# Keeping the transposed keys of a delta-rule layer for its recurrence, and giving one output half another tile's space

## The chip, the cores and the metric

The kernel runs on one core of one Trainium2 chip. The time is the device time of one execution in microseconds (us), the median of several runs. An engine is named as the profile names it: PE is the matrix engine, DVE the vector engine, ACT the scalar engine, POOL the general engine (GpSimd), SP the engine whose only work here is to issue transfers. A name with a q behind it (SPq, ACTq) is that engine's queue of transfers.

## The reference, cut to what matters

One decoder layer on 512 tokens of width 1024, all in float32. One input projection feeds two groups of heads, whose outputs go together through the output projection `w_out`; cross-attention, a SwiGLU block and a last norm follow.

```
u = rmsnorm(x) @ w_in
# group A, 4 heads of 128: q, k, v through a short convolution and silu; q, k normalised by head;
# decay g_cum and beta per token. In chunks of tokens:
a_mat = where(strict, beta * (k k^T) * decay, 0) + I          # lower triangular
u_c, w_c = solve(a_mat, [v * beta, k * beta * exp(g_cum)])
v_new = u_c - w_c state
o     = q_dec state + (q k^T * decay) v_new
state = state * last + k_dec^T v_new                          # k_dec = k * exp(g_last - g_cum)
# then a gated RMSNorm of o
# group B, 8 heads of 64: a score per (query, key), the best 128 keys of each query,
# softmax attention over those with a relative-position bias
h = x + concat(A, B) @ w_out
h = h + cross_attention(rmsnorm(h), mem);  h = h + swiglu(rmsnorm(h));  out = rmsnorm(h)
```

## The kernel before, in words

Four chunks of 128 tokens take the place of the reference's chunks of 64. Matmuls of full precision are made of three passes over pairs of a rounded tile and its rest (`wh`, `wl`, `XH`, `XL`, lines 149 to 151); most of PE's time goes to such passes.

Nobody writes an order of instructions by hand. The body is written as helpers in program order, and the tile framework runs a model of the engines over it and lays out each engine's list. So what stands next to what is decided by that planner, from the tiles that instructions read and write, and an edit of a few lines can change the lists far from where it stands. On the chip every engine takes its own list strictly in order.

PSUM, the matrix engine's output memory, has eight banks; in the first third they are divided into `g` (3 buffers), `lg` (2), `tp` (2) and `o` (1). A tile that names a `tag` shares its space with the other tiles of that tag and has to wait until they are no longer read.

The part that the change touches, group A, goes through these steps:

- `project` makes q, k and v of a head, by dense passes on PE and a convolution on DVE, ACT and POOL (lines 360 to 383). Beside it DVE runs `topk`, group B's selection: 16 rounds of a MAX8 and a MATCH_REPLACE for each of three score blocks (lines 486 and 487), then three fills (line 490).
- `prepare(h)` transposes the keys of head h on PE (`tokens`, line 634), squares them for the norm (`squares`, ACT), turns the norm into factors on POOL (`rsqrt`, whose power stands in line 234, and `kdc` in line 651), makes k k^T and q k^T on PE, and writes `NTt` and `A` on DVE (line 662). `NTt` goes to memory (line 665, `n_d`) by SP's queue.
- `diagonal_blocks` reads all 16x16 diagonal blocks back (line 678), inverts them on DVE by a chain of small operations (lines 688 to 707), writes them to `x_d` and `y_d` (line 709) and spreads them by eight transfers each into `X` and `Y` (line 714), which POOL has set to zero (lines 847 and 848).
- `level(0)`, `level(1)` and `last_level` build the full inverse from the blocks on PE and DVE (lines 723 to 755).
- `values_of` transposes the values (line 634 again) and `gates` makes the gate `zg` from the last four pairs of weights, split on POOL (line 142).
- `recurrence` goes over the chunks. Before the first it makes `ktok`, the keys with tokens in the partitions, times `kdc`: per head four transposes into the single buffer of bank `o` and one multiply on DVE (lines 765 to 769). A chunk uses `ktok` in line 778 for the state; its output is squared (line 811), scaled by POOL's power (line 234) and DVE (lines 813 to 818), transposed (line 822) and split into `OGh` and `OGl`.
- `attention` of group B runs in pairs of heads: copies `nath`, `natl` and transfers into `ks`, `kl`, `qs` (lines 562 to 572), logits (579, 580), a bias add and max (589), exp (591), transposes (595), their copy (597), then values (604) and row sums (613).

`ktok` has the tag `X`: it lies where `X` lay. `OGl` has the tag `OGl`, where `wu`, an early weight, lay. `Dm`, the decay factors that `prepare` reads, has the tag `X` too.

Of the kernel before, what the change touches and what calls it, by code (L numbers as in the profile page):

```python
# [10 lines left out]
FT = mybir.dt.float32  # L11
FR = mybir.dt.float32r
AF = mybir.ActivationFunctionType
OP = mybir.AluOpType
AX = mybir.AxisListType

T = 512
D = 1024
MEM = 256
NT = T // 128  # L20
# [61 lines left out]
def hybrid_block(ctx, tc, I, out):  # L82
    nc = tc.nc
    pe, act, dve, pool, sp = nc.tensor, nc.scalar, nc.vector, nc.gpsimd, nc.sync
# [19 lines left out]
    def pool_of(name, side=None):  # L104
        return tc.alloc_tile_pool(name=name, bufs=1, reuse_waits="tile", side=side) if side else \
            tc.alloc_tile_pool(name=name, bufs=1, reuse_waits="tile")
# [15 lines left out]
    def ps(tag="at"):  # L122
        n_ps[0] += 1
        if tag not in banks:
            turn[tag] = turn.get(tag, -1) + 1
            tag = alias[tag][turn[tag] % len(alias[tag])]
        return banks["pool"].tile([128, 512], FT, name=f"ps{n_ps[0]}", tag=tag, bufs=banks[tag])
# [5 lines left out]
    def t2k(shape=(128, 512), dt=FT):  # L133
        n_t[0] += 1
        return tmp.tile(list(shape), dt, name=f"t2k{n_t[0]}", tag="t2k", bufs=4)
# [45 lines left out]
    QK = [gdn.tile([128, 2, T], FT, name=f"QK{h}", tag=f"QK{h}") if h < 3 else None for h in range(4)]  # L181
# [45 lines left out]
    def small(n, dt=FT):  # L227
        n_small[0] += 1
        return held((128, n), f"sm{n_small[0]}", dt)
# [55 lines left out]
    for j in range(4):  # L285
        for t in range(NT):
            tt = slice(t * 128, (t + 1) * 128)
            for k in range(2):
                kk = 2 * j + k
                o = pu[t][:, :N_DSA]  # L290
# [5 lines left out]
    gp = pool_of("gp", "right")  # L296
# [12 lines left out]
    for t in range(NT):  # L309
# [17 lines left out]
        for d in range(2):  # L327
# [4 lines left out]
                          None, op0=OP.mult)  # L332
# [55 lines left out]
    for pr_ in range(4):  # L388
        q = ps()
# [48 lines left out]
    q = ps()  # L438
# [13 lines left out]
    for h in range(4):  # L452
        q = ps()
# [15 lines left out]
    q = ps()  # L469
# [151 lines left out]
        att.release()  # L621


    NTt = A = X = Y = None
    n_d = dram.tile([16 * 129, 128], FT, name="n_d")
    x_d = dram.tile([128, 256], FT, name="x_d")
    y_d = dram.tile([128, 256], FT, name="y_d")
    kdc, ssq_ = small(16), small(16)
    irk = {}

    def tokens(src, bank="g"):
        q = ps(bank)
        for c in range(NT):
            pe.transpose(q[:, c * 128:(c + 1) * 128], src[:, c * 128:(c + 1) * 128], ident)  # L634
        return q

    def squares(q, dst):
        j = t2k()
        for c in range(NT):
            act.activation(j[:, c * 128:(c + 1) * 128], q[:, c * 128:(c + 1) * 128], AF.Square,  # L640
                           accum_out=dst[:, c:c + 1])

    def prepare(h):
        hc = slice(4 * h, 4 * h + 4)
        rk, cc = small(4), small(4)
        irk[h] = small(4)
        squares(tokens(QK[h][:, 0, :]), rk)
        rsqrt(rk, rk, 1.0)
        pool.tensor_tensor(cc, rk, rk, op=OP.mult)
        pool.tensor_tensor(cc, cc, beta[:, hc], op=OP.mult)  # L650
        pool.tensor_tensor(kdc[:, hc], cc, kd[:, hc], op=OP.mult)
        dve.reciprocal(irk[h], rk)
        for c in range(NT):
            act.activation(Dm[:, h, c, :], Dm[:, h, c, :], AF.Identity, scale=cc[:, c:c + 1])
        for c2 in range(2):
            q = ps("g")
            for e in range(2):
                c = 2 * c2 + e
                pe.matmul(q[:, 256 * e:256 * e + 256], QK[h][:, 0, c * 128:(c + 1) * 128],
                          QK[h][:, :, c * 128:(c + 1) * 128], start=True, stop=True)  # L660
            for k, dst in enumerate((NTt, A)):
                dve.tensor_tensor(dst[:, h, 2 * c2:2 * c2 + 2, :],
                                  q.rearrange("p (e k i) -> p e k i", e=2, k=2)[:, :, k, :],
                                  Dm[:, h, 2 * c2:2 * c2 + 2, :], op=OP.mult)
        sp.dma_start(bass.AP(tensor=n_d.tensor, offset=n_d.offset + h * 66048,
                             ap=[[128, 128], [16512, 4], [1, 128]]), NTt[:, h])
        squares(tokens(QK[h][:, 1, :]), ssq_[:, hc])
        pool.tensor_tensor(QK[h][:, 1, :], QK[h][:, 1, :], row[:, h, :], op=OP.mult)
# [89 lines left out]
    def recurrence():  # L758

        sg, sg2 = small(16), small(16)  # L760
        rsqrt(sg, ssq_, 1.0)
        dve.tensor_scalar(sg, sg, float(np.float32(128 ** -0.5)), None, op0=OP.mult)
        dve.tensor_tensor(sg2, sg, sg, op=OP.mult)
        dve.tensor_scalar(sg2, sg2, 1.0 / 128, None, op0=OP.mult)
        ktok = gp.tile([128, 4, NT, 128], FT, name="ktok", tag="X")
        for h in range(4):
            q = tokens(QK[h][:, 0, :], "o")
            dve.tensor_tensor(ktok[:, h], q.rearrange("p (c d) -> p c d", c=NT),
                              kdc[:, 4 * h:4 * h + 4].unsqueeze(2).to_broadcast([128, NT, 128]), op=OP.mult)
        S = gp.tile([128, 4, 128], FT, name="S")  # L770
        yield
        for c in range(NT):
            cs = slice(c * 128, (c + 1) * 128)

            def heads(o, f):
                for h in range(4):
                    a_, b_ = f(h)
                    pe.matmul(o[:, h * 128:(h + 1) * 128], a_, b_, start=True, stop=True)  # L778

            Z = cv((128, 4, 128))  # L780
            O = ps("g")
            if c:
                q = ps("g")
                heads(q, lambda h: (QK[h][:, 0, cs], S[:, h, :]))

                for h in range(4):
                    pe.matmul(O[:, h * 128:(h + 1) * 128], QK[h][:, 1, cs], S[:, h, :], start=h == 0, stop=False)
                for h in range(4):
                    dve.scalar_tensor_tensor(Z[:, h, :], q[:, h * 128:(h + 1) * 128],
                                             negc[:, 4 * h + c:4 * h + c + 1], vtok[h][:, c, :], op0=OP.mult,  # L790
                                             op1=OP.add)
            q = ps("g")
            heads(q, lambda h: (Y[:, h, c, :], Z[:, h, :] if c else vtok[h][:, c, :]))
            V = cv((128, 4, 128))
            for h in range(4):
                act.activation(V[:, h], q[:, h * 128:(h + 1) * 128], AF.Copy)
            if c < NT - 1:
                q = ps("g")
                heads(q, lambda h: (ktok[:, h, c, :], V[:, h, :]))
                if c:  # L800
                    for h in range(4):
                        dve.scalar_tensor_tensor(S[:, h, :], S[:, h, :], last[:, 4 * h + c:4 * h + c + 1],
                                                 q[:, h * 128:(h + 1) * 128], op0=OP.mult, op1=OP.add)
                else:
                    dve.tensor_copy(S.rearrange("p h d -> p (h d)"), q)
            for h in range(4):
                pe.matmul(O[:, h * 128:(h + 1) * 128], A[:, h, c, :], V[:, h, :], start=not c and h == 0, stop=h == 3)
            so, fo = small(4), small(4)
            j = t2k()
            for h in range(4):  # L810
                act.activation(j[:, h * 128:(h + 1) * 128], O[:, h * 128:(h + 1) * 128], AF.Square,
                               accum_out=so[:, h:h + 1])
            dve.tensor_tensor(so, so, sg2[:, c::4], op=OP.mult)
            rsqrt(fo, so, 1.0)
            dve.tensor_tensor(fo, fo, sg[:, c::4], op=OP.mult)
            on = cv((128, 4, 128))
            for h in range(4):
                dve.scalar_tensor_tensor(on[:, h, :], O[:, h * 128:(h + 1) * 128], fo[:, h:h + 1],
                                         zg[c][:, h * 128:(h + 1) * 128], op0=OP.mult, op1=OP.mult)
            q = ps("g")  # L820
            for h in range(4):
                pe.transpose(q[:, h * 128:(h + 1) * 128], on[:, h, :], ident)
            split(OGh[:, :, cs], OGl[:, :, cs], q.rearrange("p (h i) -> p h i", h=4))
            yield
# [15 lines left out]
    xn.release()  # L840
    NTt = gp.tile([128, 4, NT, 128], FT, name="NTt", tag="NT")
    A = gp.tile([128, 4, NT, 128], FT, name="A", tag="A")
    for h in range(4):
        prepare(h)
    X = gp.tile([128, 4, NT, 128], FT, name="X", tag="X")
    Y = gp.tile([128, 4, NT, 128], FT, name="Y", tag="Y")
# [6 lines left out]
    for h in range(4):  # L853
        values_of(h)
    OGh = gp.tile([128, 4, T], FR, name="OGh", tag="NT")
    OGl = gp.tile([128, 4, T], FR, name="OGl", tag="OGl")
    core = recurrence()
    steps(core, 2)
    for i, _ in enumerate(attention()):
# [50 lines left out]
    for k in range(KD):  # L910
        q = ps()
# [138 lines left out]
    for f0, nf in ((0, 8), (8, 8)):  # L1050
        HT = [gated(f) for f in range(f0, f0 + nf)]
        for m in range(KD):
            wh, wl = weights(I["w_down"][0], f0, nf, m * 128, 128)
            o = dense(wh, wl, [a for a, _ in HT], [b for _, b in HT])
# [5 lines left out]
    for hf in range(2):  # L1060
        for t in range(NT):
            q = ps()
# [67 lines left out]
```

## Time and profile before

| | us |
|---|---|
| median of 3 runs | 844.17 (843.04 to 844.74) |
| the profiled execution | 844.85 |
| its span, first to last instruction | 843.1 |
| PE busy | 817.6 (97%) |
| DVE busy | 477.3 (57%) |
| ACT busy | 371.6 (44%) |
| POOL busy | 191.3 (23%) |

The times of the trace count from the span's start; 1.75 us of the profiled execution lie outside the span. An instruction's duration on PE includes a modelled end, so that back-to-back matmuls overlap in the list: their cost is read from one start to the next. A bracket behind a row gives how long the engine sat idle ahead of it and what ended that.

### The profile page before, as it was taken

What the parts mean: (1) busy time and instruction counts of PE and PEld (TensorE: products, weight loads), DVE (VectorE), ACT (ScalarE), POOL (GpSimd) and SP (SyncE); (2) the same over time, 40 slices, a digit from 0 to 9 for tenths busy, and PEclk for the clock granted to TensorE, in tenths of its full rate; (3) what the DMA queues carried; (4) which work ended last, traced back from release to release, by engine and by line L of the source; (5) the groups of instructions that cost most, each with busy time, mean ns of one, the idle gap of its engine ahead of it and who ended that gap; (6) DMA issues with size and microseconds to landing.
All of it is one profiled execution on the core that took longest, in us unless ns stands there. A gap on an engine that the chain in (4) does not pass through costs nothing.

```text
span 843.1 us, 11038 instructions
## 1 busy us (share of the span) xinstructions
PE 817.6 (97%) x4122; PEld 680.3 (81%) x4122; DVE 477.3 (57%) x817; ACT 371.6 (44%) x736; POOL 191.3 (23%) x202
## 2 busy tenths in 40 slices
PE   8999999879998999999999999999999999999996
PEld 7787788768886888888878888888888888888885
DVE  7779999936673654564644444544354553335542
ACT  6679767227675543453544342322233222223332
POOL 5432578662310231000003211110011110001122
PEclk9999999989999999999999999999999999999998
DMA  8541333057415334343323533323333333332202
GB/s 292 144 110 30 111 100 89 7 112 169 121 51 204 96 101 128 111 137 100 101 59 94 172 100 101 92 83 101 100 100 101 93 89 100 94 100 87 88 25 100
DMA packets 134941, 88.31 MB, mean 105 GB/s; under 512 B 10304, under 2 KB 122344, under 8 KB 134888
## 3 DMA queue, kind: packets, MB, share of 16 engines
q1 hardware_dynamic: 131848, 85.87, 35.0%
q10 hardware_dynamic: 3040, 1.75, 0.7%
q8 instruction: 32, 0.52, 0.3%
q14 instruction: 21, 0.17, 0.1%
HBM read 76.84 MB, written 4.99 MB: 97 GB/s over the span
## 4 chain that ended last, share of the span: by engine, by line
PE 87%; DVE 4%; ACT 4%; DMA 2%; issue 1%; POOL 0%; SPq 0%; POOLq 0%; DVEq 0%; ACTq 0%
PE ps L149 23%; PE ps L151 23%; PE ps L150 23%; PE ps L604 1%; PE ps L723 1%; PE ps L778 1%; PE ps L1075 1%; PE ps L1074 1%; PE ps L1073 1%; PE ps L595 1%; PE ps L951 1%; PE ps L949 1%; PE ps L950 1%; PE ps L731 1%; PE ps L634 1%
## 5 line engine op out<-in xcount | busy, mean ns | idle before, releaser
L141 ACT ACTIVATE wh<-wraw 128x1024 fp32r<-128x1024 f32 x120 | 127.2, 1061 | 322.3 <-PE ps L150 169.2
L151 PE MATMUL ps<-XH,wl 128*128 128x512 f32 x512 | 201.1, 393 | 0.0
L149 PE MATMUL ps<-XH,wh 128*128 128x512 f32 x512 | 200.4, 391 | 0.4 <-DVE cp L366 0.3
L150 PE MATMUL ps<-XL,wh 128*128 128x512 f32 x512 | 199.5, 390 | 0.0
L142 DVE TENSOR_TENSOR wl<-wraw,wh 128x1024 fp32r<-128x1024 f32 x108 | 153.7, 1424 | 68.2 <-ACT wh L141 67.9
L149 PEld LDWEIGHTS ps<-XH,wh 128*128 128x128 f32 x512 | 96.2, 188 | 20.3 <-DVE cp L366 0.8
L150 PEld LDWEIGHTS ps<-XL,wh 128*128 128x128 f32 x512 | 96.2, 188 | 20.1 <-issue 0.2
L151 PEld LDWEIGHTS ps<-XH,wl 128*128 128x128 f32 x512 | 96.1, 188 | 19.6
L1044 POOL TENSOR_TENSOR t2k<-t2k,t2k 128x512 f32<-128x512 f32 x22 | 29.4, 1335 | 291.0 <-DVE t2k L1043 281.8
L258 POOL TENSOR_TENSOR acc<-acc,t2k 128x512 f32<-128x512 f32 x21 | 36.6, 1741 | 172.5 <-ACT t2k L257 172.0
L1043 DVE TENSOR_TENSOR t2k<-ps,row 128x512 f32<-128x512 f32 x22 | 15.2, 691 | 67.9 <-PE ps L151 67.9
L151 PE MATMUL ps<-HH,wl 128*128 128x512 f32 x128 | 50.0, 393 | 0.0
L149 PE MATMUL ps<-HH,wh 128*128 128x512 f32 x128 | 49.9, 390 | 0.0
L150 PE MATMUL ps<-HL,wh 128*128 128x512 f32 x128 | 49.6, 390 | 0.0
L1055 DVE TENSOR_TENSOR XR<-ps,XR 128x512 f32<-128x512 f32 x16 | 11.1, 692 | 51.9 <-PE ps L151 51.9
L1041 DVE TENSOR_TENSOR t2k<-ps,row 128x512 f32<-128x512 f32 x22 | 15.2, 691 | 36.0 <-PE ps L151 36.0
L142 POOL TENSOR_TENSOR wl<-wraw,wh 128x1024 fp32r<-128x1024 f32 x12 | 29.0, 2420 | 15.3 <-ACT wh L141 15.3
L885 DVE TENSOR_TENSOR XR<-ps,XR 128x512 f32<-128x512 f32 x16 | 11.0, 690 | 32.1 <-PE ps L151 32.1
L150 PEld LDWEIGHTS ps<-HL,wh 128*128 128x128 f32 x128 | 24.0, 188 | 5.1
L151 PEld LDWEIGHTS ps<-HH,wl 128*128 128x128 f32 x128 | 24.0, 188 | 4.9
L149 PEld LDWEIGHTS ps<-HH,wh 128*128 128x128 f32 x128 | 24.1, 188 | 4.9
L486 DVE MAX8 m<-masks 128x8 f32<-128x512 f32 (+2 forms) x48 | 26.8, 558 | 0.9
(395 smaller groups left out, 1628.9 us busy)
## 6 DMA issues: line engine op xcount, KB each, us to landing
wraw<-in_w_gate SPq DMA_DIRECT2D x22, 512.0 KB, 3.6
wraw<-in_w_up SPq DMA_DIRECT2D x22, 512.0 KB, 3.7
wraw<-in_w_down SPq DMA_DIRECT2D x20, 512.0 KB, 3.8
wraw<-in_w_in SPq DMA_DIRECT2D x16, 512.0 KB, 3.6
wraw<-in_w_xkv SPq DMA_DIRECT2D x16, 512.0 KB, 3.8
wraw<-in_w_out SPq DMA_DIRECT2D x8, 512.0 KB, 3.9
wraw<-in_w_xq SPq DMA_DIRECT2D x8, 512.0 KB, 3.8
wraw<-in_w_xo SPq DMA_DIRECT2D x8, 512.0 KB, 3.7
```

Of the source, the lines that this page charges most:

```text
L141: act.activation(h, src, AF.Copy)
L142: (sub or dve).tensor_tensor(l, src, f32(h), op=OP.subtract)
L149: pe.matmul(o, lh, rh, start=start, stop=False)
L150: pe.matmul(o, lh, rl, start=False, stop=False)
L151: pe.matmul(o, ll, rh, start=False, stop=stop)
L258: pool.tensor_tensor(self.acc, self.acc, s_, op=OP.add)
L486: dve.max(m8, score[t])
L885: dve.tensor_tensor(XR[m], o, XR[m], op=OP.add)
L1041: dve.tensor_tensor(s1, og_, Rrow2, op=OP.mult)
L1043: dve.tensor_tensor(s2, ou_, Rrow2, op=OP.mult)
L1044: pool.tensor_tensor(s1, s1, s2, op=OP.mult)
L1055: dve.tensor_tensor(XR[m], o, XR[m], op=OP.add)
```

## The change

`prepare` keeps the transposed keys (`kt`, in bank `g`) until `kdc` is there, and multiplies them into `ktok` at once. `recurrence` no longer transposes the keys again. For that `ktok` has to be there earlier, and takes the tag `OGl`; `OGl` takes the tag `X`. Behind line 654 the changed kernel's line numbers are 3 higher than before, and behind the block that is taken out of `recurrence` 2 lower.

```diff
-    NTt = A = X = Y = None
+    NTt = A = X = Y = ktok = None
...
-        squares(tokens(QK[h][:, 0, :]), rk)
+        kt = tokens(QK[h][:, 0, :])
+        squares(kt, rk)
         rsqrt(rk, rk, 1.0)
...
         dve.reciprocal(irk[h], rk)
+        dve.tensor_tensor(ktok[:, h], kt.rearrange("p (c d) -> p c d", c=NT),
+                          kdc[:, hc].unsqueeze(2).to_broadcast([128, NT, 128]), op=OP.mult)
...
-        ktok = gp.tile([128, 4, NT, 128], FT, name="ktok", tag="X")
-        for h in range(4):
-            q = tokens(QK[h][:, 0, :], "o")
-            dve.tensor_tensor(ktok[:, h], q.rearrange("p (c d) -> p c d", c=NT),
-                              kdc[:, 4 * h:4 * h + 4].unsqueeze(2).to_broadcast([128, NT, 128]), op=OP.mult)
...
     A = gp.tile([128, 4, NT, 128], FT, name="A", tag="A")
+    ktok = gp.tile([128, 4, NT, 128], FT, name="ktok", tag="OGl")
...
-    OGl = gp.tile([128, 4, T], FR, name="OGl", tag="OGl")
+    OGl = gp.tile([128, 4, T], FR, name="OGl", tag="X")
```

The instruction counts of ACT, POOL, SP and DVE stay; PE has 16 transposes fewer. The lists are laid out anew from the first heads' `prepare` on, up to the start of `w_out`; from there PE's list is as before but for some transposes of the memory tokens, which stand earlier.

DVE around the last head's `NTt` and `A`. Before (`cv_1771` holds the diagonal blocks that have come back, `m_994` and `masks` are the selection's):

```order
L662 TENSOR_TENSOR NTt<-ps_1750,Dm 128x256
L662 TENSOR_TENSOR A<-ps_1750,Dm 128x256
L486 MAX m_994<-masks 128x8
L379 SCALAR_TENSOR_TENSOR cp_1416<-cp_1406,prT,ps_1409 128x512
L487 MATCH_REPLACE masks<-m_994,masks 128x512
L486 MAX m_994<-masks 128x8
L487 MATCH_REPLACE masks<-m_994,masks 128x384
L486 MAX m_994<-masks 128x8
L688 TENSOR_SCALAR cv_1771<-cv_1771 128x256
L487 MATCH_REPLACE masks<-m_994,masks 128x256
L486 MAX m_994<-masks 128x8
L487 MATCH_REPLACE masks<-m_994,masks 128x512
```

After, the same place (`ps_1729` holds the kept keys of head 3, `sm_920` is `kdc`, `cv_1776` holds the diagonal blocks):

```order
L654 TENSOR_TENSOR ktok<-ps_1729,sm_920 128x512
L486 MAX m_994<-masks 128x8
L665 TENSOR_TENSOR NTt<-ps_1750,Dm 128x256
L665 TENSOR_TENSOR A<-ps_1750,Dm 128x256
L665 TENSOR_TENSOR NTt<-ps_1755,Dm 128x256
L665 TENSOR_TENSOR A<-ps_1755,Dm 128x256
L487 MATCH_REPLACE masks<-m_994,masks 128x512
L486 MAX m_994<-masks 128x8
L487 MATCH_REPLACE masks<-m_994,masks 128x384
L486 MAX m_994<-masks 128x8
L487 MATCH_REPLACE masks<-m_994,masks 128x256
L486 MAX m_994<-masks 128x8
```

The last pair of `NTt` and `A` now stands behind four `ktok` multiplies, the convolution's line 379 and one round more of the selection (four MAX, three MATCH_REPLACE); behind line 691, the old 688, one round is left where there were two.

PE at the end of `level(0)`'s products. Before (`cv_1822` to `cv_1843` are the masked products of line 725, `qs_2163` and its like the queries of the first pair of attention heads):

```order
L723 MATMUL ps_1838<-X,NTt 128x128 x4
L731 MATMUL ps_1845<-Y,cv_1822 128x128 x4
L731 MATMUL ps_1851<-Y,cv_1829 128x128 x4
L731 MATMUL ps_1857<-Y,cv_1836 128x128 x4
L731 MATMUL ps_1863<-Y,cv_1843 128x128 x4
L634 MATMUL ps_1869<-cst,Y 128x128 x4
L634 MATMUL ps_1875<-cst,Y 128x128 x4
L634 MATMUL ps_1881<-cst,Y 128x128 x4
L634 MATMUL ps_1887<-cst,Y 128x128 x4
L723 MATMUL ps_1893<-X,NTt 128x128 x4
L579 MATMUL ps_2185<-kl_2163,qs_2161 128x128
L580 MATMUL ps_2185<-ks_2162,qs_2161 128x128
```

After:

```order
L734 MATMUL ps_1850<-Y,cv_1827 128x128 x4
L734 MATMUL ps_1856<-Y,cv_1834 128x128 x4
L579 MATMUL ps_2165<-kl_2143,qs_2141 128x128
L580 MATMUL ps_2165<-ks_2142,qs_2141 128x128
L734 MATMUL ps_1862<-Y,cv_1841 128x128 x4
L734 MATMUL ps_1868<-Y,cv_1848 128x128 x4
L579 MATMUL ps_2166<-kl_2143,qs_2141 128x128
L580 MATMUL ps_2166<-ks_2142,qs_2141 128x128
L634 MATMUL ps_1874<-cst,Y 128x128 x4
```

The first logits of attention have moved ahead of two products of `level(0)`, of its four groups of transposes and of the first product of `level(1)`, and with them all of attention against the inverse and the recurrence.

PE ahead of `w_out`. Before (`ps_2664` is the last chunk's output, `ps_2708` its transpose):

```order
L807 MATMUL ps_2664<-cv_2683,A 128x128 x4
L595 MATMUL ps_2856<-cst,sm_2_2852 128x128 x3
L595 MATMUL ps_2871<-cst,sm_3_2867 128x128 x4
L595 MATMUL ps_2881<-cst,sm_3_2877 128x128 x4
L604 MATMUL ps_2887<-PT_2769,vt_980 64x512
L613 MATMUL ps_2899<-cst,c_3_2796 64x128 x8
L604 MATMUL ps_2887<-PT_2772,vt_980 64x512
L604 MATMUL ps_2887<-PT_2769,vt_984 64x384
L604 MATMUL ps_2887<-PT_2772,vt_984 64x384
L604 MATMUL ps_2887<-PT_2769,vt_988 64x256
L822 MATMUL ps_2708<-cst,cv_2703 128x128 x3
L604 MATMUL ps_2887<-PT_2772,vt_988 64x256
```

After (`ps_2644` is the last chunk's output, `ps_2688` its transpose):

```order
L776 MATMUL ps_2658<-cv_2643,Y 128x128 x4
L604 MATMUL ps_2867<-PT_2749,vt_980 64x512
L613 MATMUL ps_2879<-cst,c_3_2776 64x128 x8
L604 MATMUL ps_2867<-PT_2752,vt_980 64x512
L604 MATMUL ps_2867<-PT_2749,vt_984 64x384
L604 MATMUL ps_2867<-PT_2752,vt_984 64x384
L604 MATMUL ps_2867<-PT_2749,vt_988 64x256
L805 MATMUL ps_2644<-cv_2663,A 128x128 x4
L604 MATMUL ps_2867<-PT_2752,vt_988 64x256
L604 MATMUL ps_2867<-PT_2749,vt_992 64x128
L604 MATMUL ps_2867<-PT_2752,vt_992 64x128
L820 MATMUL ps_2688<-cst,cv_2683 128x128 x4
```

In both lists `w_out`'s line 149 follows within five rows. The last chunk's output product (line 807, now 805) has moved behind five of the last pair's eight value products.

## Rows read from the trace of the kernel before

**Rows 1.** The page's busy times: engine, busy us, share of the span, instructions.
```profile
PE 817.6 (97%) x4122; PEld 680.3 (81%) x4122; DVE 477.3 (57%) x817; ACT 371.6 (44%) x736; POOL 191.3 (23%) x202
```

**Rows 2.** Windows: us of each engine (instructions), granted clock, share of DMA engines, GB/s.
```profile
120.00:140.00 20.00, 20.00 (x96) 16.62 (x95) 18.93 (x48) 13.60 (x37) 15.26 (x17) 1.00 0.33 93
```

**Rows 3.** Waits from 155 to 266 us: who waited for what, us, times, longest.
```profile
PE ps L723 <- DMA B<-tb_d: 5.6, 1, 5.6
PE ps L595 <- ACT PT L597: 1.5, 1, 1.5
PE ps L595 <- ACT sm L591: 1.4, 2, 1.0
```

**Rows 4.** Timeline of PE, level 0: start, us, line, tiles, count, [idle before].
```profile
177.44 6.51 PE L723 MATMUL ps<-X,NTt 128*128 128x128 f32 x32 [5.62 <-DMA B<-tb_d]
183.79 3.74 PE L731 MATMUL ps<-Y,cv 128*128 128x128 f32 x32
```

**Rows 5.** Timeline of DVE from the last `A` to the end of the blocks' inverse.
```profile
144.44 0.41 DVE L662 TENSOR_TENSOR A<-ps,Dm 128x256 f32<-128x256 f32 x1
...
149.93 1.24 DVE L688 TENSOR_SCALAR cv<-cv 128x256 f32<-128x256 f32 x1 [1.46 <-DMA cv<-n_d]
...
151.59 0.70 DVE L486 MAX8 m<-masks 128x8 f32<-128x512 f32 x1
...
155.35 0.69 DVE L486 MAX8 m<-masks 128x8 f32<-128x512 f32 x1
...
157.67 2.33 DVE L695 TENSOR_TENSOR cv<-cv,cv 128x12 f32<-128x12 f32 x1
...
160.44 1.88 DVE L692 TENSOR_TENSOR cv<-cv,cv 128x16 f32<-128x16 f32 x1
...
163.32 0.15 DVE L692 TENSOR_TENSOR cv<-cv,cv 128x12 f32<-128x12 f32 x1
...
168.99 0.39 DVE L707 COPY cv<-cv 128x256 f32<-128x256 f32 x1
```

**Rows 6.** Timeline of POOL in the same stretch.
```profile
144.11 2.42 POOL L142 TENSOR_TENSOR wl<-wraw,wh 128x1024 fp32r<-128x1024 f32 x1 [1.69 <-ACT wh L141]
...
154.45 2.92 POOL L234 TENSOR_TENSOR sm<-sm,mhalf 128x16 f32<-128x16 f32 x1
157.33 4.95 POOL L142 TENSOR_TENSOR wl<-wraw,wh 128x1024 fp32r<-128x1024 f32 x2
```

**Rows 7.** Timeline of SP's queue: time spent issuing.
```profile
169.03 0.34 SPq L709 DMA_DIRECT2D x_d<-cv  x1
...
170.77 4.29 SPq L714 DMA_DIRECT2D X<-x_d  x8
```

**Rows 8.** The same queue later: the first pair's queries.
```profile
185.07 1.18 SPq L571 DMA_DIRECT2D qs<-nath  x2
187.98 1.10 SPq L572 DMA_DIRECT2D qs<-natl  x2
```

**Rows 9.** Timeline of PE: the transposes for `ktok` and what follows them.
```profile
207.35 0.66 PE L634 MATMUL ps<-cst,QK 128*128 128x128 f32 x4 [0.27 <-DVE ktok L768]
...
211.10 0.66 PE L634 MATMUL ps<-cst,QK 128*128 128x128 f32 x4
211.51 0.36 PE L579 MATMUL ps<-kl,qs 128*128 128x256 f32 x1
```

**Rows 10.** Instructions on the tile `ktok`: durations min/median/max in ns, starts.
```profile
L768 DVE TENSOR_TENSOR ktok<-ps,sm x4: 676/692/692, 206.6 to 213.8; 128x512 f32<-128x512 f32 x4
```

**Rows 11.** Timeline of ACT, third chunk's end: squares of its output.
```profile
242.30 0.28 ACT L811 ACTIVATE t2k<-ps 128x128 f32<-128x128 f32 x1 [0.30 <-PE ps L807]
```

**Rows 12.** Timeline of DVE, third chunk's end: its output is scaled.
```profile
245.26 1.12 DVE L818 SCALAR_TENSOR_TENSOR cv<-ps,sm,zg 128x128 f32<-128x128 f32 x4
```

**Rows 13.** Windows behind PE's waits for the last pair.
```profile
258.00:260.00 2.00, 2.00 (x10) 0.90 (x12) 1.29 (x5) 0.60 (x1) 0.47 (x1) 0.55 1.07 363
260.00:262.00 2.00, 2.00 (x16) 1.59 (x15) 0.00 (x0) 0.53 (x1) 0.00 (x0) 0.60 0.97 355
```

**Rows 14.** Timeline of PE ahead of `w_out`.
```profile
252.80 1.05 PE L807 MATMUL ps<-cv,A 128*128 128x128 f32 x8
...
264.49 0.50 PE L149 MATMUL ps<-odh,wh 128*128 128x512 f32 x1
```

## The prediction

> **What bounds the kernel now.** I read the page's busy times first: PE works for 97% of the span and no other engine for more than 57% [rows 1]. So the time is PE's work plus the few places where PE waits or runs at the low clock, and an edit is worth what it does to those. The list of PE's waits comes next. In the stretch that the change lays out anew it has one large entry, 5.6 us at the first product of `level(0)`, and two of 1.5 and 1.4 us in the last pair of attention heads [rows 3]. The third view is the timeline around the large one: PE sits for 5.62 us and starts at 177.44 [rows 4]. Its releaser is given as a transfer of `B`, but eight transfers into `X` were issued just ahead of it on the same queue [rows 7]; what PE needs is `X`, and `X` is the end of a chain on DVE. So up to 177.44 us DVE sets the time and not PE. DVE is full there: 18.93 of 20 us between 120 and 140 us [rows 2]. From 177.44 us to the start of `w_out` at 264.49 us [rows 4, 14] PE sets the time again, with few gaps. Behind 264.49 PE's list is dense and stays.
>
> The sum thus has two parts: when `level(0)` starts, and how much PE work, waiting and low clock lies between that and `w_out`. I work it against the profiled execution, 844.85 us, which is 0.68 above the median of 844.17; a difference of a sum is carried over to the median as it is.
>
> **The transposes that go.** There are 16, in four groups of four. The first group ran before the wait at 177.44, where PE has time to spare: nothing gained. Three groups ran behind it. From the start of one to the next instruction is 0.41 us [rows 9], so 3 x 0.41 = 1.23 us, all on PE's path. One of the three waited 0.27 us for the multiply ahead of it, since bank `o` has one buffer [rows 9]; that goes too. Together -1.5 us.
>
> **The multiplies that move.** Four of about 0.69 us each [rows 10] leave the stretch from 206 to 214 us, where DVE has time, and go into the selection's, where it has none. The order has them all ahead of the last head's `NTt` and `A`, and with them one convolution step of about the same size and one more round of the selection. A round takes 155.35 - 151.59 = 3.76 us [rows 5]; a fourth MAX of 0.7 us comes with it. Together 4 x 0.65 (their spacing when queued, an estimate just under their duration) + 0.7 + 3.76 + 0.7 = 7.8 us, so the last `A` would end at 144.85 + 7.8 = 152.6 us. The low bound takes off what DVE idled, about 1 us in each 20 [rows 2] and some 3 us in all: 149.6. The high bound counts two rounds, the multiply and the four last products behind the last projection's eviction: about 155.
>
> Behind the last `A` the chain is shorter than before. Then: 144.85 to 168.99 + 0.39 = 169.38, or 24.5 us [rows 5]. Now: 5.1 us until the blocks are back (149.93 - 144.85), 1.24 for line 688, one round and three fills for some 3.9 us, since the other round is already done, and then the inversion without a round between its steps. From 163.32 to 169.38 it took 6.1 us, and the four small steps ahead of that need 0.1 each, 6.4 together. Sum 16.6 us. So the chain ends at 152.6 + 16.6 = 169.2 instead of 169.38: -0.2 us, with bounds of -3.2 and +2.6. The transfers behind it are the same, and two of `B` that now stand ahead of those into `X` on SP's queue fit into the 1.4 us in which that queue waits for `x_d` to land (169.37 to 170.77 [rows 7]). That these two shifts nearly cancel is the main point of the sum, and luck.
>
> Two of the chain's steps on a dozen numbers took 2.33 and 1.88 us, while the same step later took 0.15 [rows 5]. Both end when POOL's two weight splits end, 157.33 + 4.95 = 162.28 [rows 6]. My 6.4 us leaves such blocking out. In the new order one weight split follows `X`'s zeroing and the power of 2.92 us [rows 6] is last; counted from the last `A`, POOL is through about 11 us later, when the inversion has just begun. With blocking for as long as the power the chain would be 2.9 us later.
>
> The Trainium skill, "SBUF — State Buffer", section "SBUF: two separate sides", says that a DVE operation with two SBUF inputs and a GpSimd operation that reads SBUF exclude one another for a whole instruction. Rows 5 and 6 agree: 2.33 us for a dozen numbers. By it the zeroing of `X` and `Y` would block nothing and only the power's end could: up to 0.8 us more on the sum, against none in mine.
>
> **Waits that are new in `level(0)`.** PE now meets the first logits behind the second of the four products of line 734. For them the first pair's `ks`, `kl` and `qs` must have landed. PE gets there at about 177.2 + 6.5 + half of 3.74 = 185.6 us [rows 4]. In the run before, the queue issued `qs` at 185.07 and 187.98 us [rows 8]. Those issues waited for `natl` on DVE, which the new order puts earlier, behind the second masked product of line 728. After the eight of `X`, which end at 175.06, twelve transfers at about 0.6 us each [rows 8] could be out at 182.3, and landed before PE arrives. If the old times hold, PE waits until 187.98 + 1.1 + a landing, some 3.5 us or more. Behind the waiting logits stand two more products of line 734, and DVE's subtractions behind those. I take 1.0 us, nearer to the early case; bounds 0 and +4. No saving is possible here, as PE was not idle.
>
> **The end, ahead of `w_out`.** Before, the last chunk's product of line 807 ran at 252.80 us, 11.7 us ahead of `w_out` [rows 14], and its squares, power, scaling and transposes lay beside the last pair's attention. Now it stands behind five of that pair's eight value products, and three short ones are left to cover what follows. The chain's price is read at the third chunk: squares from 242.30, scaled at 245.26 + 1.12 = 246.38, or 4.1 us [rows 11, 12]. The three products cover about 0.3 us, so PE is idle for some 3.8 us just ahead of `w_out`. On the other side, the last pair loses the squares from ACT's list ahead of its copies `PT`, for which PE waited 1.5 us [rows 3], and part of the low clock goes: at 0.55 and 0.60 of full speed (1.2 GHz for most of it), four microseconds behind PE's waits lost 2 x 0.45 + 2 x 0.40 = 1.7 us [rows 13]. I take half of that as saved at the old place and a little as lost at the new one: 3.8 - 1.5 - 1.0 = +1.3 us. Low bound -1.5, if ACT comes to the squares so early that the value products, at the low clock, cover the chain; high bound +5.5, if nothing is saved and `w_out` starts at the low clock after the new gap.
>
> Giving `OGl` the space of `X` costs nothing: `last_level` is the last to read `X`, and the first chunk's output comes many steps later. `ktok` in the space of `wu` costs nothing either: `wu` is read by `latents`, before the first `prepare`. The kept `kt` holds one of three buffers of `g` until POOL has made `kdc`; PE may wait for it, but it does so ahead of 177.44, where 5.6 us are spare.
>
> **The sum.** -1.5 - 0.2 + 1.0 + 1.3 = +0.6 us on 844.85, so 845.4 for such an execution, and 844.17 + 0.6 = 844.8 for the median.
>
> **The rivals.**
>
> The gaps do not open, and the change gives back what it takes out. `level(0)` starts early (half of its bound, -1.6), the transposes go (-1.5), `qs` is there in time (0) and the squares get in early (-1). For it: every engine but PE has time behind 177 us. Against it: two of these gaps stand in the order, and PE can't pass a waiting instruction. -4.1 us: 840.1.
>
> The last chunk's chain is wholly bare. PE idles 3.8 us ahead of `w_out` and pays 1.7 us of low clock behind it, the waits for the last pair stay, and `level(0)` waits 1 us: -1.5 - 0.2 + 1.0 + 5.5 = +4.8, 849.0. It decides for slower from the point where the covered part of the 4.1 us, and of the 1.5 us and 1.7 us that I take as saved, falls below about 2 us together. For it: the order at the end. Against it: ACT and DVE are nearly free there.
>
> The moved multiplies make DVE's chain late. This is the case in which the new place is worse by itself: 2.6 us of work on a full engine, ahead of what sets 177.44. If `level(0)` starts at the high bound, +2.6, the sum is +3.4, 847.6. Against it: half of the selection's rest has moved ahead too and shortens what follows.
>
> **Chances.** This kernel's measurement can't tell less than about 0.2%, 1.7 us, from no change. The forecast has 0.38; its own range is 842.7 to 846.8. The first rival, faster, has 0.26. The second has 0.24, the third 0.12. Nearly all of the forecast's share counts as no change (0.28), with 0.04 below and 0.06 above; of the rivals 0.01, 0.02 and 0.02 fall within. That gives faster 0.29, same 0.33, slower 0.38. The range of 8 in 10 reaches from 841.0, most of the way to the first rival, to 849.0, the second.
>
> **What would show it right or wrong.** The first product of `level(0)` within 2 us of 177.4, DVE's last `A` near 152.6 and line 710 near 169 us: the cancelling is right. A wait of line 579 for a transfer in `level(0)` of 0 to 2 us. A wait of line 820 for DVE just ahead of `w_out` of 2 to 4 us, and `w_out` at 264.5 + 0.6 us. I am wrong if `level(0)` starts more than 3 us off, if line 820 finds its input ready, or if the trace behind `w_out`'s start is not the same length as before.

## The result and the profile after

The changed kernel takes 853.9 us (median of 4 runs, 851.44 to 855.21), the kernel before 843.95 us beside it (4 runs, 843.04 to 844.74). The ratio is 1.0113, 95% interval 1.0101 to 1.0125: it is slower by 9.95 us, outside the range of 841 to 849. A second set on another occasion gave 1.0116 (1.0097 to 1.0134).

The profiled execution is the longest of the four (855.21 us); its span is 853.4 us, 10.3 more than before. Two marks divide the difference. `level(0)` starts 6.1 us later, and `w_out` another 2.3 us; the last 1.9 us come behind the start of `w_out`. First the list of PE's waits from 60 to 290 us (who waited for what: us, times, longest), beside [rows 3]:

```profile
PE ps L726 <- DMA X<-x_d: 15.9, 1, 15.9
PE ps L820 <- DVE cv L816: 4.7, 3, 2.9
PE ps L595 <- ACT sm L591: 1.1, 2, 0.9
```

The large wait has gone from 5.6 to 15.9 us, and a wait for the scaled chunk output is new. PE's busy time is as before, 817.8 us here. The timeline of PE at the two marks, beside [rows 4, 14]:

```profile
183.55 6.46 PE L726 MATMUL ps<-X,NTt 128*128 128x128 f32 x32 [15.93 <-DMA X<-x_d]
...
267.12 1.16 PE L805 MATMUL ps<-cv,A 128*128 128x128 f32 x8
...
271.95 1.25 PE L820 MATMUL ps<-cst,cv 128*128 128x128 f32 x4 [2.88 <-DVE cv L816]
272.86 0.77 PE L149 MATMUL ps<-odh,wh 128*128 128x512 f32 x1
```

`level(0)` starts at 183.55 instead of 177.44, `w_out` at 272.86 instead of 264.49. The windows right behind it (us of each engine, granted clock third from the end) show PE at half the clock there, 1.2 GHz, where before (first row) it ran at full clock:

```profile
264.00:266.00 2.00, 2.00 (x12) 1.45 (x12) 1.29 (x2) 1.20 (x2) 0.00 (x0) 1.00 1.04 423
```
```profile
272.00:274.00 2.00, 2.00 (x7) 1.57 (x8) 0.80 (x4) 0.76 (x2) 0.00 (x0) 0.50 0.59 227
274.00:276.00 2.00, 2.00 (x7) 1.52 (x6) 0.56 (x1) 2.00 (x7) 0.00 (x0) 0.50 0.00 0
```

There is a second such stretch, at the end of the second chunk, behind a wait of line 820 of 1.26 us:

```profile
244.00:246.00 2.00, 2.00 (x12) 2.00 (x11) 0.87 (x5) 0.00 (x0) 0.00 (x0) 0.50 0.40 120
```

Now the chain that sets `level(0)`, on DVE, beside [rows 5]. Lines 691 to 710 are the old 688 to 707:

```profile
152.65 0.42 DVE L665 TENSOR_TENSOR A<-ps,Dm 128x256 f32<-128x256 f32 x1
...
158.99 1.63 DVE L691 TENSOR_SCALAR cv<-cv 128x256 f32<-128x256 f32 x1 [2.29 <-DMA cv<-n_d]
...
161.79 1.13 DVE L490 TENSOR_SCALAR masks<-masks 128x512 f32<-128x512 f32 x1
...
164.80 0.16 DVE L695 TENSOR_TENSOR cv<-cv,cv 128x12 f32<-128x12 f32 x1
...
165.84 1.15 DVE L698 TENSOR_TENSOR cv<-cv,cv 128x12 f32<-128x12 f32 x1
167.02 2.54 DVE L703 TENSOR_TENSOR cv<-cv,cv 128x64 f32<-128x64 f32 x2
...
172.58 1.67 DVE L706 TENSOR_TENSOR cv<-cv,cv 128x512 f32<-128x512 f32 x1
...
175.00 0.37 DVE L710 COPY cv<-cv 128x256 f32<-128x256 f32 x1
```

The last `A` is there at 153.07 (152.6 was predicted). But from it to the end of line 710 at 175.37 go 22.3 us, where 16.6 were worked out. Steps that cost 0.17 us elsewhere cost 1.15, and 0.45 became 2.54. POOL in the same stretch, beside [rows 6]:

```profile
158.01 2.40 POOL L142 TENSOR_TENSOR wl<-wraw,wh 128x1024 fp32r<-128x1024 f32 x1
...
160.82 1.81 POOL L847 MEMSET Y<- 128x2048 f32 x1
162.60 3.07 POOL L234 TENSOR_TENSOR sm<-sm,mhalf 128x16 f32<-128x16 f32 x1
165.64 3.80 POOL L511 TENSOR_TENSOR zg<-zg,brow 128x512 f32<-128x512 f32 x3
...
172.06 1.26 POOL L511 TENSOR_TENSOR zg<-zg,brow 128x512 f32<-128x512 f32 x1
```

The three gain multiplies on `zg` run from 165.64 to 169.44. The slow step of line 698 starts 0.2 us behind the start of the first of them, and the two of line 703 end 0.1 us behind the end of the third. The slow step of line 706 starts inside the fourth multiply, which ends at 173.32, and is done 0.9 us later. Before, the same multiplies came behind the inverse, since ACT made `zg` only then:

```profile
173.38 2.48 POOL L511 TENSOR_TENSOR zg<-zg,brow 128x512 f32<-128x512 f32 x2 [11.10 <-ACT zg L509]
```

That row is of the kernel before: POOL had been waiting 11.1 us for ACT's `zg`. The transfers behind the chain did not change: from line 710's end to PE's start 8.2 us now, 8.1 before.

### The profile page after: what moved, and what is told of

Same layout as the page of the kernel before. It is cut to its first block, busy times and chain, and to the rows that moved or that the text cites. A ratio compares the mean times of both kernels' runs of the same rounds, so it can differ in the third digit from the quotient of the medians.

```text
span 853.4 us, 10998 instructions
## 1 busy us (share of the span) xinstructions
PE 817.8 (96%) x4106; PEld 680.4 (80%) x4106; DVE 477.2 (56%) x817; ACT 370.8 (43%) x736; POOL 193.9 (23%) x202
## 4 chain that ended last, share of the span: by engine, by line
PE 84%; DVE 6%; ACT 3%; issue 2%; POOL 2%; DMA 2%; SPq 0%; POOLq 0%; DVEq 0%; ACTq 0%
PE ps L149 22%; PE ps L150 22%; PE ps L151 22%; PE ps L604 1%; PE ps L726 1%; PE ps L1074 1%; PE ps L1073 1%; PE ps L1072 1%; PE ps L776 1%; PE ps L948 1%; PE ps L950 1%; PE ps L949 1%; PE ps L595 1%; DMA X<-x_d 1%; POOL sm L234 1%
## 5 line engine op out<-in xcount | busy, mean ns | idle before, releaser
L1054 DVE TENSOR_TENSOR XR<-ps,XR 128x512 f32<-128x512 f32 x16 | 11.1, 691 | 51.8 <-PE ps L151 51.8
L588 POOL TENSOR_TENSOR bm<-masks,B 128x256 f32<-128x256 f32 x24 | 18.1, 771 | 43.2 <-DVE c L589 27.4
```

The lines of the kernel that those rows point to most:

```text
L588: pool.tensor_tensor(bm[:, n - 256:], score[t][:, n - 256:], BT[s], op=OP.add)
L1054: dve.tensor_tensor(XR[m], o, XR[m], op=OP.add)
```

## The experiments

Nine runs, all beside runs of the kernel before (843.8 to 844.1 us). Theory A: POOL's work in SBUF holds up the inverse on DVE. Theory C: the new end ahead of `w_out` costs time by itself.

**late_gain: the gain multiplies wait for the inverse.**

```diff
-            pool.tensor_tensor(s..., s..., gdn_b..., op=OP.mult)        # in gates()
...
+    gain = held((128, 128), "gain")                                     # behind diagonal_blocks()
+    act.activation(gain, gdn_b, AF.Identity, scale=one_of[0])           # Yb[:, 0, 0:1]
+    for s in zg:
+        pool.tensor_tensor(s..., s..., gain..., op=OP.mult)
```

The diffs of this section are shortened; dots stand for what is left out.

> The changed kernel, but POOL's four gain multiplies on zg read a copy of the gain that ACT makes from an element of Yb (always 1), so they can't start before the blocks' inverse is done. The lists of PE, DVE and SP stay word for word. Theory A (POOL's SBUF-to-SBUF work holds up DVE's two-operand steps of the inverse): the steps 698, 703 and 706 that took 1.15, 2.54 and 1.67 us while POOL ran the gain multiplies lose part of that; POOL's six mask copies now come to stand there and may hold them for up to 2.7 us; first to last step of the inverse 7 to 9.5 us instead of 10.6, level 0 at 180 to 182.5 us instead of 183.55, time 850 to 852.5. Rival B (the steps are slow because they stand in a row, each waiting for the one before, and start late): 10 to 10.6 us, level 0 at 183 to 184, time 853 to 855.

Measured: 850.19 us, ratio 1.0068 (1.0052 to 1.0085). The first and the last step of the inverse, and POOL beside them:

```profile
163.82 0.16 DVE L694 TENSOR_TENSOR cv<-cv,cv 128x12 f32<-128x12 f32 x1
...
170.65 0.38 DVE L709 COPY cv<-cv 128x256 f32<-128x256 f32 x1
```
```profile
164.65 1.99 POOL L546 COPY bm<-masks 128x128 f32<-128x128 f32 x6
171.54 4.94 POOL L852 TENSOR_TENSOR zg<-zg,gain 128x512 f32<-128x512 f32 x4 [4.90 <-ACT gain L850]
```

From the first to the last step the inverse takes 7.2 us (163.82 to 171.03) instead of 10.6, with the lists of PE, DVE and SP unchanged, and `level(0)` starts at 179.28 (180 to 182.5 expected). Theory A holds. `level(0)` gained 4.3 us, of which about 1 us is an earlier last `A` that the edit does not explain: places far ahead of any edit vary by about that much between profiled executions.

**late_gain2: the mask copies go to ACT as well.**

```diff
-                pool.tensor_copy(b_[:, :128 * t - 128], score[t][:, :128 * t - 128])
+                act.activation(b_[:, :128 * t - 128], score[t][:, :128 * t - 128], AF.Copy)
```

> As the run before, and the six mask copies are on ACT instead of POOL, so that POOL has nothing to do during the inverse. Theory A: the inverse takes 6.5 to 7.2 us, level 0 starts at 179.5 to 180.3, time 849.5 to 851. Rival B: 10 to 10.6 us, 183 to 184, time 853 to 855. What is then left over 844 (some 6 us) would lie in the start of the inverse and in the end ahead of w_out.

Measured: 847.9 us, 1.0057 (1.0036 to 1.0078); a second set (late_gain2_again, below) 848.94 us. DVE's timeline, the same steps as above (lines 694 to 709 here):

```profile
164.13 0.17 DVE L694 TENSOR_TENSOR cv<-cv,cv 128x12 f32<-128x12 f32 x1
...
165.17 0.17 DVE L697 TENSOR_TENSOR cv<-cv,cv 128x12 f32<-128x12 f32 x1
165.37 0.45 DVE L702 TENSOR_TENSOR cv<-cv,cv 128x64 f32<-128x64 f32 x2
...
168.50 1.07 DVE L705 TENSOR_TENSOR cv<-cv,cv 128x512 f32<-128x512 f32 x1
...
170.33 0.38 DVE L709 COPY cv<-cv 128x256 f32<-128x256 f32 x1
```

1.15 became 0.17, 2.54 became 0.45, 1.67 became 1.07: 6.6 us instead of 10.6, with DVE's, PE's and SP's lists word for word those of the changed kernel. So 4.0 of the 5.7 us by which the chain was mis-sized are POOL's work beside the inverse. By late_gain 3.4 of them are the gain multiplies; the other 0.6 went with the mask copies. `level(0)` starts at 178.65 (179.5 to 180.3 expected). The time fell by 5 to 6 us; the gain in front of `level(0)` is 4.9. The expectation, 849.5 to 851, was too high by about 1.6 us for the first set and 0.6 us for the second. What is left, some 4 us, was expected at the start of the inverse and at the end.

**tags_only: the two places alone.**

```diff
-        ktok = gp.tile([128, 4, NT, 128], FT, name="ktok", tag="X")
+        ktok = gp.tile([128, 4, NT, 128], FT, name="ktok", tag="OGl")
-    OGl = gp.tile([128, 4, T], FR, name="OGl", tag="OGl")
+    OGl = gp.tile([128, 4, T], FR, name="OGl", tag="X")
```

> The kernel before with the two tags alone: ktok in the space of wu and OGl in that of X; ktok is still made in the recurrence by its own transposes. The lists up to level 0 stay; behind it the planner lays out an order in which the last chunk's output product stands behind five of the last pair's value products, as in the changed kernel. Theory C (the changed end costs time by itself): level 0 at 177.4 us, PE waits 2 to 3 us for the last scaled output ahead of w_out and starts w_out at the low clock, time 846 to 849. Rival D (all of the loss is in front of level 0): time 843 to 845.

Measured: 848.28 us, 1.0055 (1.0040 to 1.0071). The gap that theory C expects ahead of `w_out` is there, and from 270 to 272 us PE runs at a granted clock of 0.50:

```profile
268.38 1.10 PE L822 MATMUL ps<-cst,cv 128*128 128x128 f32 x4 [2.88 <-DVE cv L818]
269.23 0.48 PE L149 MATMUL ps<-odh,wh 128*128 128x512 f32 x1
```

But the run does not separate the end from what lies ahead of `level(0)`, as was expected of it: the lists change there too. The three groups of `ktok`'s transposes that ran behind `level(0)`'s start now stand ahead of it, and so do all four multiplies of line 768 on DVE, one of them in the middle of the inverse. POOL's first split, from 158.57 us on, also holds a fill that took 0.41 us before:

```profile
158.60 2.61 DVE L490 TENSOR_SCALAR masks<-masks 128x512 f32<-128x512 f32 x1
161.13 2.34 DVE L695 TENSOR_TENSOR cv<-cv,cv 128x12 f32<-128x12 f32 x1
...
168.78 0.68 DVE L768 TENSOR_TENSOR ktok<-ps,sm 128x512 f32<-128x512 f32 x1
```

`level(0)` starts at 179.56 us, 2.1 late: 1.3 us come with a later last `A`, up to which the lists are the same, and 1.0 us with a longer inverse, of which 0.1 is made up behind it. The profiled execution is one of the two longest of six (850.9 us); of its 6.0 us over the kernel before, 3.9 lie behind `level(0)`'s start. The two places by themselves cost 4.2 us by the medians; how much of that is the end stays open. They are no add-on to the early `ktok` but its condition, since the space of its old tag `X` still holds `Dm` while `prepare` runs.

**ktok_act: the kept keys are multiplied on ACT.**

```diff
-        dve.tensor_tensor(ktok[:, h], kt..., kdc[:, hc]..., op=OP.mult)
+        for c in range(NT):
+            act.activation(ktok[:, h, c, :], kt[:, c * 128:(c + 1) * 128], AF.Identity,
+                           scale=kdc[:, 4 * h + c:4 * h + c + 1])
```

> The changed kernel with the multiplies of the kept keys on ACT (four of 128x128 a head, the factor as scale) instead of DVE. Theory E (2.6 us of work on a full DVE makes the last A late): the last A ends 2 to 2.7 us earlier than 153.1, level 0 some 2 us earlier, time 848 to 852; the gain multiplies still meet the inverse. Rival F (DVE's gaps would have taken them): last A within 0.7 us of 153.1, time 853 to 855 but for the end. In this order the last chunk's product stands ahead of all eight value products, so by theory C the wait ahead of w_out falls to 0 to 1.5 us, a further 2 us.

Measured: 842.7 us (12 runs), 0.9979 (0.9965 to 0.9994): faster than before by 0.2%, and far below the 848 expected. From its timelines of DVE, POOL and PE:

```profile
145.50 0.42 DVE L666 TENSOR_TENSOR A<-ps,Dm 128x256 f32<-128x256 f32 x1
...
158.80 2.36 DVE L490 TENSOR_SCALAR masks<-masks 128x384 f32<-128x384 f32 x1
161.08 2.64 DVE L704 TENSOR_TENSOR cv<-cv,cv 128x64 f32<-128x64 f32 x2
```
```profile
158.59 4.82 POOL L142 TENSOR_TENSOR wl<-wraw,wh 128x1024 fp32r<-128x1024 f32 x2
```
```profile
176.68 6.66 PE L727 MATMUL ps<-X,NTt 128*128 128x128 f32 x32 [5.43 <-DMA X<-x_d]
...
258.26 1.06 PE L806 MATMUL ps<-cv,A 128*128 128x128 f32 x8
...
263.97 0.66 PE L821 MATMUL ps<-cst,cv 128*128 128x128 f32 x4
264.38 0.48 PE L149 MATMUL ps<-odh,wh 128*128 128x512 f32 x1
```

Theory E was right in its direction and wrong in its size: the last `A` comes 7.2 us earlier, not 2 to 2.7, because the planner also puts a round of the selection behind it again. All lists are new from the first `prepare` on, so the run does not single out what the 2.6 us of multiplies cost. The gates end late again, and it is the weight splits, not the gain multiplies, that hold DVE: a fill of line 490 (2.36 us, 0.33 in the kernel before) beside the first, and a step of the inverse beside the second, which ends at 163.41. At the end there is no gap of note ahead of line 821.

**act_late_split: ktok_act, and the last gate weights are split behind the inverse.**

```diff
+                act.activation(wh, raw, AF.Identity, scale=one_of[0])         # j == 3 only
+                dve.tensor_tensor(wl, raw, f32(wh), op=OP.subtract)
...
     diagonal_blocks()
+    for _ in gg:                                                          # the rest of gates()
+        pass
```

> The kept keys multiplied on ACT as in ktok_act, and the last pair of gate weights is split only when the blocks' inverse is done: its rounded half on ACT with an element of Yb (always 1) as scale, its rest on DVE instead of POOL. Theory A (POOL's two-operand work in SBUF holds up the inverse): in ktok_act one step took 2.64 instead of 0.45 us beside two weight splits of POOL that ended at 163.4; with one split gone that falls to at most 0.5 us, the inverse ends 1.5 to 2.5 us earlier, the last gate products fill PE's wait for X, level 0 at 174.5 to 176, time 839.5 to 842. Rival G (PE's last gate products, now behind the inverse, come too late and push level 0): level 0 at 177 to 180, time 843 to 846.

Measured: 839.45 us, 0.9954 (0.9937 to 0.9971): the fastest version, 4.4 us below the kernel before. DVE and POOL, then PE:

```profile
162.23 0.44 DVE L714 TENSOR_TENSOR cv<-cv,cv 128x64 f32<-128x64 f32 x2
...
167.85 0.38 DVE L721 COPY cv<-cv 128x256 f32<-128x256 f32 x1
```
```profile
159.74 2.35 POOL L142 TENSOR_TENSOR wl<-wraw,wh 128x1024 fp32r<-128x1024 f32 x1
```
```profile
169.46 1.53 PE L513 MATMUL ps<-wh,XH 128*128 128x512 f32 x4 [2.51 <-ACT wh L507]
...
176.71 3.73 PE L738 MATMUL ps<-X,NTt 128*128 128x128 f32 x32
```

The step of 2.64 us takes 0.44, by theory A. `level(0)` starts no earlier (176.71, against 174.5 to 176 expected). In this execution the last `A` was 1.2 us later than in ktok_act's; and PE no longer waits for `X` but goes on from the last gate product, so a part of rival G holds. With the 8.1 us that the transfers took before, `X` would be there at 176.3 us (an estimate), so at most 0.4 us hang on the products. What was not expected is the clock. PE now works through what was its wait, and the first product of `level(0)` runs at full clock, 3.73 us instead of 6.5.

**before_late_split: the same split in the kernel before.**

> The kernel before with the last pair of gate weights split after the inverse in the same manner, ktok unchanged. Theory A: the two steps of 2.33 and 1.88 us beside POOL's two weight splits lose half of that or more (one split is left, and ends 2.4 us earlier); the inverse ends 1.5 to 3 us earlier, level 0 at 174.5 to 176; but the planner lays the end out with the last chunk's product behind fewer value products, wait of line 833 0.5 to 2 us; time 841 to 844. Rival G: level 0 at 177 to 180, time 844 to 847.

Measured: 843.37 us (842.2 to 852.96, two of the twelve runs at 853), 1.0011 (0.9984 to 1.0039): no difference that can be told. The hold is seen again on DVE:

```profile
157.91 2.32 DVE L705 TENSOR_TENSOR cv<-cv,cv 128x12 f32<-128x12 f32 x1
...
160.68 0.16 DVE L702 TENSOR_TENSOR cv<-cv,cv 128x16 f32<-128x16 f32 x1
```

Of the two held steps in [rows 5] the one beside the split that is left stays at 2.32 us, and the one beside the split that is gone falls from 1.88 to 0.16. The inverse ends 1.4 us earlier, `level(0)` starts 1.1 us earlier, straight behind the gate products, and runs at full clock. Nearly all of it is given back behind: between `level(0)` and `w_out` PE idles 87.56 - 81.65 = 5.9 us in this kernel and 87.06 - 83.25 = 3.8 in the one before (length less busy time of the two stretches), the most of it in line 589 waiting for DVE (2.9 us) and in line 833 (1.6 us).

**cover and late_gain2_again: work in the gap.** Into late_gain2 go 16 transposes whose result nobody reads.

```diff
+            if pr_ == 3:
+                q = ps("tp")
+                for i in range(16):
+                    pe.transpose(q[:, (i % 4) * 128:(i % 4 + 1) * 128], on[:, ...], ident)
```

> late_gain2 with 16 more transposes on PE, of the last pair's output, whose result nobody reads; they stand between the last value product and the last chunk's transposes, so that PE works in the gap of 2.9 us ahead of w_out. All other lists stay. Theory H (the gap's larger price is the low clock that may follow it): 16 x 0.11 us of work fit into the gap and cost nothing, the gap splits into about 1 and 0.3 us, w_out starts at full clock, the time falls below late_gain2's by 1 to 3 us and varies less (846 to 848). Rival I (the gap costs only its own length, and the clock is lowered by something else): same time as late_gain2 or up to 0.5 us more, w_out at the low clock as often as there.

> The same kernel as late_gain2, beside cover on one chip: 846.9 to 852, at the mean clock 0.985 to 0.992, the longer times at the lower clock.

Measured: cover 847.76 us (846.88 to 848.82), late_gain2_again 848.94 us (845.91 to 851.19). In PE's timeline of cover the gap is filled, and `w_out` starts at full clock:

```profile
264.24 1.97 PE L621 MATMUL ps<-cst,on 128*128 128x128 f32 x16 [0.85 <-DVE on L616]
266.27 1.11 PE L824 MATMUL ps<-cst,cv 128*128 128x128 f32 x4
267.13 0.48 PE L149 MATMUL ps<-odh,wh 128*128 128x512 f32 x1
```

More work on the engine that bounds the kernel did not make it slower, and no run of cover is above 848.82, where 5 of the 12 runs of late_gain2 are above 849; those ran at a mean clock of 0.984 to 0.987, all others of both kernels at 0.988 or more. That speaks for theory H and does not show it: that none of 5 runs is among the 5 longest of 17 comes about by chance about one time in eight. The size speaks less for it: the medians differ by 0.1 and 1.2 us, at or below the low end of what was expected, and with these runs I can't give it better. In five of the six profiled executions with a gap of 2.9 us the clock falls to 0.50 in the gap or within 2 us behind it. The exception is late_gain's, with the same gap of 2.88 us and `w_out` at full clock; it took 846.89 us, the other five runs of late_gain 849.47 to 850.79.

**after_again: the changed kernel once more.**

> The changed kernel itself beside the same runs of before, for the size of what late_gain and late_gain2 take away and to see how often w_out starts at the low clock: 851 to 855, level 0 at 182 to 184.5, the inverse 10 to 11 us.

Measured: 853.86 us (850.47 to 854.77), the inverse from 164.91 to 175.49 (10.6 us), `level(0)` at 183.51, as expected.

## Why the prediction was wrong, point by point

The sum had -0.2 us for the start of `level(0)` and -1.5 + 1.0 + 1.3 = +0.8 for what lies behind it. The profiled execution shows +6.1 and +4.2. So the mechanism of the first part failed, and the second was mis-sized.

- **The transposes that go**, -1.5 us: not measured alone. Nothing speaks against it, and it was far too small to matter.
- **The multiplies that move.** The last `A` at 152.6 was right within 0.5 us.
- **The chain behind the last `A`**: this step failed. It ended at 175.37 us, 6.0 later than before, where -0.2 was worked out, with +2.6 as the high bound. "My 6.4 us leaves such blocking out" was the wrong end to take. I had seen that POOL's weight splits held two steps in the kernel before, moved the splits out of the way, and did not ask what POOL would do next. Its list has the gain multiplies right behind the power, and their input, ACT's `zg`, came later than the inverse before. There POOL split the last two weights behind the power, from 157.33 to 162.28 us, PE waited 2.5 us in that stretch and ran at a clock of 0.67 from 160 to 164; which of these made the gates late, no run separates. In the new order PE's gate products end at 167 instead of 172 us, `zg` is early, and the multiplies fall into the inverse. late_gain shows 3.4 us for them, late_gain2 4.0 with the mask copies. A further 0.8 us came with the read-back of the blocks (5.9 instead of 5.1 us), and 0.7 us in lines 691 and 490 beside POOL's split and its zeroing; those two are read from the trace and were not tested. The read-back itself may not be the cause: in after_again the blocks were back after 5.3 us, line 691 then took 2.30 us, and in both executions it ended 0.2 us behind POOL's split. The two transfers of `B` had 0.9 us of the queue and not 1.4, since `y_d` is issued until 169.84 us; that cost 0.2 us at most (the first transfer into `X` goes out 1.9 us behind that of `x_d`, 1.7 before).
- **"That these two shifts nearly cancel is the main point of the sum, and luck."** They don't cancel: +8.2 us for the last `A`, and only 2.2 us of it won back.
- **Waits that are new in `level(0)`**, +1.0 us: 0 in the trace. Line 579 starts at 191.55 without a wait for a transfer. But `level(0)` came 6 us late, so the race was not put to the test; in the runs where it starts at about 179 us (late_gain, late_gain2 and its second set) PE idled 0 to 0.5 us at that place.
- **The end**, +1.3 us: the mechanism was right and its size was wrong. The gap ahead of line 820 is 2.9 us (3.8 predicted). The wait for `PT` is gone as worked out. The low clock that I took as half saved came back elsewhere: behind a wait of line 820 at the second chunk's end PE ran at 0.50 from 244 to 246 us and at 0.72 up to 248, where before that chunk's end had 1.00. I had looked only at the last chunk; the waits of line 820 at the ends of earlier chunks make 1.8 us, against 0.3 before. And the low clock behind `w_out`'s start I took only as "a little", although the bound of +5.5 had it. From `level(0)` to `w_out` the changed kernel needs 2.3 us more, though 1.5 us of work and waiting is gone, and behind `w_out` 1.9 us more: 5.7 us, just above the high bound. tags_only shows the same gap, and a low clock behind it, without the kept keys; it gives no size for the end alone.
- **The rivals.** The second (849.0) and the third (847.6) each got a chance of its own as if only one could happen. Both of their outcomes came, a bare end and a late `level(0)`, with one root, the new order. The second's mechanism is the one that was seen. The third's is not: DVE's last `A` was where the forecast had it, and `level(0)` was late because POOL held the chain behind it, which no rival had. The sum of their prices over the forecast, 4.2 + 2.8, is 7.0, on 844.8 some 851.8, still 2.1 us below the measured median.

## What to carry to other kernels

When an edit makes one engine's work end earlier, go down the lists of the other engines from there and ask what its consumers will run into: here an earlier gate put POOL's multiplies into the middle of a latency-bound chain on DVE. Where a planner orders the instructions, an edit's first effect is the new order, and it is to be tried in small variants (ACT instead of DVE for the new multiply turned +1.1% into -0.2%, and one split moved out of the chain made it -0.5%). An idle stretch of the matrix engine may cost more than its length, because what follows may run at half the clock (0.50 behind `w_out`'s start here); useful work from elsewhere belongs into it.

## What the runs showed of the hardware that was not expected

- POOL's power on 128x16 took 3.07 us (161.93 to 165.0 us in late_gain2), and DVE's two-operand steps beside it, at 164.13 to 164.96 us, took 0.17 us each, as in the stretch without POOL. So it did not hold them, and the 2.9 us that I allowed for it were no bound. The Trainium skill, "SBUF — State Buffer", section "SBUF: two separate sides", has the lock held for the whole instruction; the trace agrees for the multiplies and splits (2.54, 2.33, 2.64 us) and not for the power. The profile's spans on POOL are rough, but in the changed kernel POOL's next instruction starts 3.04 us behind the power's start; why the power holds nothing, no run shows.
- POOL's zeroing of `Y` (160.82 to 162.63 us) stood beside a fill of DVE that took 1.13 us instead of 0.41 (line 490). In all six profiled executions of this order that fill ends 0.3 us behind the zeroing. Splits hold operations with one input too: line 691 ends 0.2 us behind the split in the same six. So an operation that only writes can hold one of DVE's with one input. The Trainium skill, "SBUF — State Buffer", section "SBUF: two separate sides", has a DVE operation in a two-port mode exclude a GpSimd operation, and says that `tensor_scalar`, the kind of both lines, can enter such a mode; the trace agrees, and no row shows the mode itself.
- POOL's six mask copies stood in late_gain in the place of the gain multiplies, and the inverse took 7.2 us with them and 6.6 without: 0.6 us for 2.0 us of copies, from one execution each.
